# A two-layer trunk on one core: conditioning units ahead of the output units, and a first feed-forward unit on scaled x

## The chip, the core and the metric

The kernel runs on one core of a Trainium2 chip. The metric is the time of one launch in microseconds of the device (us), as the median of several runs. The profiles are single executions recorded by the hardware profiler. Five engines appear in them: PE (TensorE: matrix products; PEld is its weight load), DVE (VectorE), ACT (ScalarE), POOL (GpSimd) and SP (SyncE), which here only issues DMA transfers.

## What is computed

256 tokens of width 1024 pass through two layers. Each has a mixer and a feed-forward part, both behind an RMS norm that is modulated by a conditioning vector `c`, both added to the residual through a gate. The conditioning of a layer is one vector-matrix product, `silu(c) @ ada_w`, cut into six pieces.

```
mod = (silu(c) @ ada_w + ada_b); sh1, sc1, g1, sh2, sc2, g2 = split(mod, 6)
even layer:
  h = rms_norm(x, norm_mix) * (1 + sc1) + sh1
  a_val, a_gate, b_x, b_gate = split(h @ w_in, 4)
  ya = silu(layer_norm(conv31(a_val * sigmoid(a_gate))))     # causal, per channel
  yb = rg_lru(conv4(b_x)) * gelu(b_gate)                     # gated linear recurrence
  x = x + g1 * (concat(ya, yb) @ w_out)
  h = rms_norm(x, norm_ffn) * (1 + sc2) + sh2
  x = x + g2 * ((silu(h @ wg) * (h @ wu)) @ wd)              # width 2816
odd layer:
  short gated convolution and attention as mixer, then
  8 experts (width 3584), the best 2 of each token, as feed-forward
```

## The kernel before

All data is fp32. The tokens lie along the free dimension: `x` is [128 partitions, 8 blocks, 256 tokens]. The activations stay on the chip; what the DMA brings is weights, 469 MB in all.

**Weights come as a stream.** `stream_plan` (L56) lists all dense weights as units of 1 MB ([128, 2048]) in the order of their use: `cols` units (256 output columns of a projection), `rows` units (256 input rows), and conditioning units. SP issues one DMA a unit into a ring of ten buffers (`raw`; seven more come in for the experts). A buffer is given free when the unit that lay in it has been used, and only then the transfer for the unit ten places further down the plan can start. `S.step` takes the next unit of the plan, `S.take` hands out a prepared one, `S.prefetch(n)` prepares n units ahead, `S.look` is the number that `take` keeps prepared.

**Units are prepared in one of three ways.** Most are split into a high and a low part that PE can multiply at its fast rate (`part`, L368): ACT casts 512 columns to a high part (L375), DVE subtracts it from the weight for the low part (L376), into seven pairs of part buffers, four pairs a unit; a product is then three (L526 to L528: high by high, high by low, low by high). The units named in `WHOLE` are multiplied in fp32 as they lie (L549, L566), which the profile records as two matmuls a product. Conditioning units are of two kinds: `ada` ones are reduced on DVE (L476), `adap` ones on PE (L499, against `silu(c)`; fp32, so two records each), whose result, a row, is turned into columns by `turned_col` (L508): a copy on ACT, a transpose and an addition on DVE (L513, L514, L519).

**The order on each engine** is that of a scheduler: an instruction is placed as soon as its inputs allow, by the order of the code and by priorities (`high_priority`); each engine then runs its own list in order. `issue_after` ties an instruction behind another.

**The even mixer, where the change lies.** The input projection fills the blocks of the four branches (L549). The 31-tap convolution runs on two engines: 13 taps of a tile of 128 channels as products with diagonal matrices on PE (`conv_pe`, L834, diagonals made by ACT in L833), 18 on DVE (L846 to L850). The gates of the recurrence are products (L942), then ACT computes tanh, exp and square root (L945 to L952, L923, L925) and DVE multiplies and scans (`lru`, L920 to L930). `layer_norm_a` (L965) sums the convolution's four blocks over channels on PE (L968), centres them on DVE (L970), squares them on ACT (L627), sums again on PE (L611), takes the root, and broadcasts the scale over partitions on PE (L600); then it normalizes and splits (L979 to L982). The output projection has a half for the recurrence (32 products, L566, not dependent on the layer norm) and a half for the normed convolution (L526 to L528). Between the two halves stand twelve `adap` units (the pieces g1, sh2, sc2). `residual` (L709) adds each finished pair of blocks to x (L725), squares it and sums the squares on PE (L611).

**The even feed-forward.** `modulate` (L630) takes the root, broadcasts the norm's scale (L600), here with six further products that only keep PE busy (L595), and for each block multiplies on DVE (L656), scales and shifts on ACT (L657), casts on ACT (L660) and subtracts on DVE (L665). The loop at L1008 runs eleven times over a gate unit, an up unit and, one turn later, a down unit.

**The class `Early` (L669)** is used before the change at one place, the odd mixer's input. It uses that the norm's scale is one number a token and can be multiplied in after the product: `add` makes high and low parts of x times the column scale (ACT L683, DVE L684), `start` multiplies them with a weight unit while the norm's scale is still being computed (with two more columns for the shift, so 258 instead of 256), and `end` multiplies the product by the scale and adds the shift's part (L702 to L706).

**The experts.** Tokens are sorted by expert; groups of 32 rows, two or three groups an expert (`NGS`). `gather` fetches the rows of coming experts by products with a 0/1 matrix (L1449) while an earlier expert is being computed.

## Time and profile before

| | us |
|---|---|
| median of 3 runs (lowest, highest) | 1328.75 (1328.02, 1328.91) |
| the profiled execution, in all | 1330.99 |
| its span in the profile | 1329.2 |
| busy in it: PE, DVE, ACT | 1267.0, 466.4, 302.0 |
| granted clock of PE, mean share of full speed | 0.987 |

The profiled execution is 2.24 us longer than the median, and 1.8 us of it lie outside the span. Stages on its clock: input projection and conditioning until about 72 us, rest of the even mixer until 142, even feed-forward until 342, odd mixer until about 478, experts to the end. Where an engine's row shows "idle before", the name behind the arrow is what ended the idle time. The chain of waits is followed back from the last instruction; a piece in it is on the path that set the end.

### The profile page before, as it was taken

How to read it: one execution, taken by the hardware profiler on the slowest of the kernel's cores; microseconds unless marked ns; L12 is line 12 of the kernel's file. 1: busy time of each engine (PE TensorE's matmuls, PEld its weight loads, DVE VectorE, ACT ScalarE, POOL GpSimd, SP SyncE). 2: the span in 40 equal slices, each digit the busy share in tenths (PEclk: the TensorE clock that was granted, in tenths of full speed). 3: DMA queues.
4: the chain of work that ended last, by engine and by line, in shares of the span. 5: the costliest groups of instructions: out<-in, count | busy, mean ns of one | idle time of the engine just before them, and what ended most of it. 6: DMA issues, size and time to landing. Idle time of an engine off the chain costs nothing.

```text
span 1329.2 us, 30372 instructions
## 1 busy us (share of the span) xinstructions
PE 1267.0 (95%) x13194; PEld 755.7 (57%) x13194; DVE 466.4 (35%) x1025; ACT 302.0 (23%) x620; POOL 1.2 (0%) x23
## 2 busy tenths in 40 slices
PE   6979999999999999999989999999979999999975
PEld 5867899999988963453324453355313354345321
DVE  5894888888868431001011000101101101100100
ACT  3272654544746432000002000002001000100000
POOL 0000000000000000000000000000000000000000
PEclk8999899999999999999999999999999999999999
DMA  9936989898510769999999999999999999999995
GB/s 384 379 136 264 419 330 347 332 346 316 199 45 1 306 269 360 408 417 416 417 419 417 416 418 417 416 418 417 416 419 419 415 417 419 397 417 417 406 417 222
DMA packets 72220, 472.23 MB, mean 355 GB/s; under 512 B 8208, under 2 KB 10256, under 8 KB 27792
## 3 DMA queue, kind: packets, MB, share of 16 engines
q1 hardware_dynamic: 72080, 470.22, 87.8%
q8 instruction: 105, 1.72, 0.5%
q14 instruction: 35, 0.29, 0.1%
HBM read 469.14 MB, written 1.05 MB: 354 GB/s over the span
## 4 chain that ended last, share of the span: by engine, by line
PE 75%; DMA 20%; ACT 2%; DVE 2%; issue 1%; SPq 0%; ACTq 0%; DVEq 0%
DMA raw<-in_moe 20%; PE acc L1529 15%; PE mm L1529 14%; PE mm L1550 8%; PE mm L527 5%; PE mm L526 4%; PE mm L528 4%; PE mm L549 4%; PE acc L528 3%; PE acc L526 3%; PE acc L527 3%; PE acc L1550 3%; PE mm L499 1%; PE acc L566 1%; PE mm L1449 1%; PE acc L1543 1%
## 5 line engine op out<-in xcount | busy, mean ns | idle before, releaser
L1529 PE MATMUL acc<-raw,xe 128*32 128x512 f32 (+1 forms) x2688 | 259.2, 540 | 3.3 <-DMA raw<-in_moe 3.3
L1529 PE MATMUL mm<-raw,xe 128*32 128x512 f32 (+1 forms) x2688 | 257.8, 540 | 3.8 <-DMA raw<-in_moe 3.8
L1529 PEld LDWEIGHTS mm<-raw,xe 128*32 128x32 f32 x2688 | 86.5, 110 | 168.7 <-issue 154.4
L1529 PEld LDWEIGHTS acc<-raw,xe 128*32 128x32 f32 x2688 | 85.7, 110 | 164.0 <-issue 149.5
L376 DVE TENSOR_TENSOR wl<-raw,wh 128x512 fp32r<-128x512 f32 x204 | 136.3, 688 | 45.2 <-ACT wh L375 36.0
L375 ACT CAST wh<-raw 128x512 fp32r<-128x512 f32 x204 | 124.3, 621 | 115.5 <-PE mm L527 72.0
L527 PE MATMUL mm<-hlo,wh 128*128 128x256 f32 x496 | 141.2, 285 | 0.1
L526 PE MATMUL mm<-hh,wh 128*128 128x256 f32 x496 | 140.6, 284 | 0.0
L528 PE MATMUL mm<-hh,wl 128*128 128x256 f32 x496 | 140.1, 283 | 0.0
L1550 PE MATMUL mm<-raw,wh 128*32 128x256 f32 x2016 | 109.3, 379 | 0.0
L527 PEld LDWEIGHTS mm<-hlo,wh 128*128 128x128 f32 x496 | 94.9, 191 | 1.3 <-issue 0.9
L526 PEld LDWEIGHTS mm<-hh,wh 128*128 128x128 f32 x496 | 94.9, 192 | 1.0 <-issue 1.0
L528 PEld LDWEIGHTS mm<-hh,wl 128*128 128x128 f32 x496 | 94.8, 191 | 1.0 <-issue 1.0
L1665 DVE TENSOR_TENSOR wl<-wl,acc 128x512 f32<-128x512 f32 (+1 forms) x22 | 13.1, 597 | 226.5 <-PE acc L1529 226.5
L1550 PEld LDWEIGHTS mm<-raw,wh 128*32 128x32 f32 x2016 | 65.5, 110 | 43.9 <-issue 1.2
L476 DVE SCALAR_TENSOR_TENSOR raw<-raw,crow 128x1024 f32<-128x1024 f32 x64 | 77.5, 1219 | 1.9 <-DMA raw<-in_wst 1.9
L1665 DVE TENSOR_TENSOR wl<-wl,mm 128x512 f32<-128x512 f32 (+1 forms) x20 | 12.0, 598 | 188.4 <-PE mm L1529 188.4
L1550 PE MATMUL acc<-raw,wh 128*32 128x256 f32 x1344 | 72.9, 379 | 0.0
L1543 PE MATMUL acc<-raw,wh 128*32 128x512 f32 x448 | 53.0, 597 | 11.6 <-DMA raw<-in_moe 11.6
L1550 PEld LDWEIGHTS acc<-raw,wh 128*32 128x32 f32 x1344 | 43.7, 110 | 29.3 <-issue 0.8
L1662 ACT ACTIVATE wl<-mm 128x512 f32<-128x512 f32 (+1 forms) x22 | 12.0, 544 | 172.0 <-PE mm L1529 172.0
L1662 ACT ACTIVATE wl<-acc 128x512 f32<-128x512 f32 (+1 forms) x20 | 10.9, 544 | 171.9 <-PE acc L1529 171.9
(359 smaller groups left out, 1300.6 us busy)
## 6 DMA issues: line engine op xcount, KB each, us to landing
raw<-in_moe SPq DMA_DIRECT2D x236, 1024.0 KB, 19.8
raw<-in_wst SPq DMA_DIRECT2D x109, 1024.0 KB, 7.0
raw<-in_moe SPq DMA_DIRECT2D x128, 768.0 KB, 15.2
raw<-in_moe SPq DMA_DIRECT2D x8, 512.0 KB, 14.5
x<-in_xt SPq DMA_DIRECT2D x1, 1024.0 KB, 5.4
out<-x SPq DMA_DIRECT2D x4, 256.0 KB, 3.5
gw<-in_gates SPq DMA_DIRECT2D x1, 512.0 KB, 19.7
mask<-in_const SPq DMA_DIRECT2D x1, 192.0 KB, 5.0
```

Of the source, the lines that this page charges most:

```text
L375: self.nc.scalar.copy(h, t[:, j:j + PART])
L376: self.nc.vector.tensor_tensor(l, t[:, j:j + PART], h.bitcast(F32), op=OP.subtract)
L476: nc.vector.scalar_tensor_tensor(src, src, 1.0, crow, op0=OP.mult, op1=OP.mult, accum_out=raw_mod[pre][:, 2 * n + b:2 * n + b + 1])
L526: nc.tensor.matmul(o, wh, xh, start=first, stop=False, skip_group_check=skip)
L527: nc.tensor.matmul(o, wh, xl, start=False, stop=False, skip_group_check=skip)
L528: nc.tensor.matmul(o, wl, xh, start=False, stop=last, skip_group_check=skip)
L549: nc.tensor.matmul(o, wh, xh[:, k], start=(cb == 0 and k == 0), stop=(k == KB - 1), skip_group_check=True)
L1529: nc.tensor.matmul(ps[j * GROUP:(j + 1) * GROUP, :width], xe[:, k, r * GROUP:(r + 1) * GROUP], w[:, j * width:(j + 1) * width], start=(k = ...
L1543: nc.tensor.matmul(yb[0][t * GROUP:(t + 1) * GROUP], hs[r], w[:, f * D + h * 512:f * D + (h + 1) * 512], start=first, stop=last, skip_grou ...
L1550: nc.tensor.matmul(yb[c // 2][t * GROUP:(t + 1) * GROUP, c % 2 * 256:c % 2 * 256 + 256], hs[r], w[:, f * D + q * 256:f * D + q * 256 + 256 ...
L1662: nc.scalar.activation(h.bitcast(F32)[:, :width], ps[:, :width], AF.Silu)
L1665: nc.vector.tensor_tensor(h, h, ps[:, :width], op=OP.mult)
```

## The change

It has six parts. The twelve `adap` units stand ahead of the four output units in the plan and are taken ahead of `layer_norm_a`, and the splits of the two last output units are issued behind the centring. `turned_col` uses tiles of another name. In the first norm, the statistics are tied behind two of the first four `adap` units. The PE part of the convolution's last tile is issued after the recurrence. `Early` is used at the even mixer's end as well: the first gate unit is multiplied by scaled x, and the loop's first turn takes its result; the six warming products go. In the experts, the gather issued in expert 0 fetches the rows of expert 1 alone, and the later ones are shifted by one (before: 1 and 2, 3 and 4, 5 and 6, 7; after: 1, 2 and 3, 4 and 5, 6 and 7).

```diff
@@ stream_plan
     plan += [_cols("e_w_in", lo) for lo in (256, 768, 1024, 1280, 1536, 1792)]
+    plan += [("adap", "e", n) for n in range(4, 16)]
     plan += [_rows("e_w_out", lo) for lo in (512, 768, 0, 256)]
-    plan += [("adap", "e", n) for n in range(4, 16)]
@@ turned_col
-        t0 = turn_pool[0].tile([P, 512], F32, name="turn0")[:, :w]
-        t1 = turn_pool[0].tile([P, 512], F32, name="turn1")[:, :w]
+        t0 = turn_pool[0].tile([P, 2, T], F32, name="sg", bufs=2).rearrange("p b t -> p (b t)")[:, :w]
+        t1 = turn_pool[0].tile([P, 2, T], F32, name="sg", bufs=2).rearrange("p b t -> p (b t)")[:, :w]
@@ even mixer, first norm
-        sq = ev.tile([P, KB, T], F32, name="ri")
+        sq = ev.tile([P, KB, T + 2], F32, name="ri")[:, :, :T]
...
         st = Stats(ones_d, 1)
-        st.add(sq[:, 0])
+        for _ in range(2):
+            S.step()
+        with tc.issue_after(ada_last[0].ins):
+            st.add(sq[:, 0])
...
-        for _ in range(4):
+        for _ in range(2):
             S.step()
@@ even mixer, gates of the recurrence (g == 0)
-                conv_pe(3)
...
                 lru()
+                conv_pe(3)
                 S.pump(1000)
@@ layer_norm_a and the output projection
-                nc.vector.scalar_tensor_tensor(cv[:, b], ps[:, :T], -1.0 / MIX, cv[:, b],
-                                               op0=OP.mult, op1=OP.add)
+                centred = nc.vector.scalar_tensor_tensor(cv[:, b], ps[:, :T], -1.0 / MIX, cv[:, b],
+                                                         op0=OP.mult, op1=OP.add)
...
-
+            return centred
+
+        for _ in range(12):
+            S.step()
+        S.look = 0
+        S.prefetch(2)
         with tc.high_priority(offset=HIGH):
-            layer_norm_a()
-        S.prefetch(4)
-        S.look = 0
+            centred = layer_norm_a()
+        with tc.issue_after(centred.ins):
+            S.prefetch(4)
         banks = [acc_bank() for _ in range(4)]
         for g in range(2):
             proj_out(banks, None, None, 0, "e_w_out", g == 0, False, ge[:, 2 * g:2 * g + 2])
-        while S.plan[S.done][0] == "adap":
-            S.step()
         for g in range(2):
             if g == 1:
-                res, st = residual(banks, "e", 2, ev)
+                S.look = 2
+                first = Early(((ev, "ri"), (ev, "xsl")), "e", "e_norm_ffn", 3, 4)
+                res, st = residual(banks, "e", 2, ev, early=first)
             proj_out(banks, yh, yl, 2 * g, "e_w_out", False, g == 1 and res)
+        first.start("e_ffn_wg")
@@ even feed-forward
-        hh, hlo, _ = modulate(ff, st, "e", "e_norm_ffn", 3, 4, warm=WARM[0])
+        hh, hlo, rt = modulate(ff, st, "e", "e_norm_ffn", 3, 4)
...
-            pg = proj_in(hh, hlo, "e_ffn_wg", 0 if c else 4)
+            pg = proj_in(hh, hlo, "e_ffn_wg") if c else first.end(ff, rt)
...
-            pu = proj_in(hh, hlo, "e_ffn_wu")
+            pu = proj_in(hh, hlo, "e_ffn_wu", 0 if c else 4)
@@ experts
-    for e in range(0, NE - 1, 2):
-        gather(e, [n for n in (e + 1, e + 2) if n < NE])
+    gather(0, [1])
+    for e in range(1, NE - 1, 2):
+        gather(e, [e + 1, e + 2])
```

PE, around the layer norm's statistics and the broadcast of its scale (L600), before. `ge,raw` are the output projection's recurrence half, `raw,cact` conditioning, `ones_m,xr` statistics.

```order
L566 MATMUL acc<-ge,raw 128x256 x3
L968 MATMUL mm<-cv,one_pp 128x256
L566 MATMUL acc<-ge,raw 128x256 x4
L611 MATMUL mm<-ones_m,xr 128x1 x4
L566 MATMUL acc<-ge,raw 128x256
L611 MATMUL mm<-ones_m,xr 128x1 x2
L566 MATMUL acc<-ge,raw 128x256
L611 MATMUL mm<-ones_m,xr 128x1 x2
L566 MATMUL acc<-ge,raw 128x256 x6
L600 MATMUL mm<-sm_o,rs_788 128x128 x2
L566 MATMUL acc<-ge,raw 128x256 x17
L499 MATMUL mm<-raw,cact 32x512 x32
```

The same place after. L600 is again the broadcast.

```order
L499 MATMUL mm<-raw,cact 32x256 x9
L611 MATMUL mm<-ones_m,xr 128x1 x2
L499 MATMUL mm<-raw,cact 32x256 x2
L566 MATMUL acc<-ge,raw 128x256
L611 MATMUL mm<-ones_m,xr 128x1 x2
L566 MATMUL acc<-ge,raw 128x256
L611 MATMUL mm<-ones_m,xr 128x1 x2
L566 MATMUL acc<-ge,raw 128x256
L611 MATMUL mm<-ones_m,xr 128x1 x2
L566 MATMUL acc<-ge,raw 128x256 x6
L600 MATMUL mm<-sm_o,rs_892 128x128 x2
L566 MATMUL acc<-ge,raw 128x256 x23
```

Ahead of the broadcast stood 15 of the 32 output products and all conditioning behind the other 17; now 9 output products stand ahead and 23 behind, and the conditioning is all ahead.

DVE, from the even mixer's last residual to the first multiplication of the normal path (L656), before. `wl` are low parts of weights, `rs` the norm's scale.

```order
L725 SCALAR_TENSOR_TENSOR x<-acc,mod_e,x 128x256 x4
L376 TENSOR_TENSOR wl<-raw,wh 128x512 x2
L476 SCALAR_TENSOR_TENSOR raw,raw_e<-raw,crow 128x1024
L579 RECIPROCAL rs_1143<-rs_1143 128x2
L376 TENSOR_TENSOR wl<-raw,wh 128x512
L583 SCALAR_TENSOR_TENSOR rs_1143<-rs_1143 128x1 x2
L476 SCALAR_TENSOR_TENSOR raw,raw_e<-raw,crow 128x1024
L588 SCALAR_TENSOR_TENSOR rs_1143<-rs_1143 128x2
L476 SCALAR_TENSOR_TENSOR raw,raw_e<-raw,crow 128x1024
L656 TENSOR_TENSOR xr<-x,mm 128x256 x4
```

The same place after. `xsl` is the low part of the scaled x, `eb` the column of the shift's part, copied from the PSUM bank that the first feed-forward unit is summed in.

```order
L684 SCALAR_TENSOR_TENSOR xsl<-x,am,ri 128x256
L588 SCALAR_TENSOR_TENSOR rs_1253<-rs_1253 128x2
L684 SCALAR_TENSOR_TENSOR xsl<-x,am,ri 128x256 x2
L376 TENSOR_TENSOR wl<-raw,wh 128x512 x3
L704 COPY eb<-mm 128x1
L656 TENSOR_TENSOR xr<-x,mm 128x256 x4
L704 COPY eb<-mm 128x1
L376 TENSOR_TENSOR wl<-raw,wh 128x512
L665 TENSOR_TENSOR hlo<-xr,hh 128x256 x2
```

Between the norm's scale and L656 stood conditioning (L476); now the scaled x, three weight splits and the copy L704 stand there, which needs the finished first unit.

## Rows read from the trace of the kernel before

**Rows 1.** Stages: length; busy PE, PEld, DVE, ACT, POOL; PEclk; DMA share; GB/s.

```profile
72.00:102.00 30.00, 20.25 (x86) 16.46 (x84) 30.00 (x66) 20.41 (x35) 0.00 (x0) 0.90 0.21 74
142.20:151.15 8.95, 5.80 (x32) 5.66 (x32) 8.16 (x20) 3.41 (x10) 0.00 (x0) 0.58 1.01 416
361.00:442.00 81.00, 80.78 (x556) 68.24 (x554) 57.10 (x147) 42.66 (x102) 0.11 (x1) 0.98 0.13 47
478.00:600.00 122.00, 122.00 (x1552) 56.99 (x1552) 16.11 (x47) 14.48 (x34) 0.00 (x0) 1.00 0.96 382
600.00:678.00 78.00, 73.35 (x731) 24.57 (x734) 8.13 (x17) 3.73 (x9) 0.00 (x0) 1.00 1.01 417
```

**Rows 2.** Chain that ended last, 102 to 153 us: start, length, what.

```profile
102.04 0.96 PE mm L968 x2
...
110.55 7.34 PE acc L566 x34
117.89 9.59 PE mm L499 x112
...
128.62 1.00 PE mm L499 x16
...
142.23 0.88 DVE x L725 x2
...
147.74 1.20 PE mm L600 x4
...
152.40 0.21 PE mm L527
```

**Rows 3.** Timeline of PE, 72 to 112: start, length, instructions, idle before and releaser.

```profile
71.69 5.78 PE L834 MATMUL acc<-ya,dg 128*128 128x256 f32 x26
...
85.67 4.91 PE L549 MATMUL mm<-hh,raw 128*128 128x256 f32 x22
99.14 2.90 PE L566 MATMUL acc<-ge,raw 128*128 128x256 f32 x6 [8.56 <-issue]
```

**Rows 4.** Timeline of DVE, 98 to 128.

```profile
101.86 1.90 DVE L376 TENSOR_TENSOR wl<-raw,wh 128x512 fp32r<-128x512 f32 x3
...
125.58 0.71 DVE L514 STREAM_TRANSPOSE turn<-turn 128x512 f32<-128x512 f32 x1 [10.76 <-ACT turn L513]
```

**Rows 5.** Timeline of ACT, 72 to 98.

```profile
72.38 3.79 ACT L833 ACTIVATE dg<-sm_o,cwa 128x128 f32<-128x128 f32 x9
...
79.83 1.28 ACT L949 ACT_TABLE_LOAD   x1
81.12 0.60 ACT L949 ACTIVATE q<-ri,lah 128x256 f32<-128x256 f32 x1
```

**Rows 6.** Timeline of PE, first two feed-forward units and the third's start.

```profile
151.15 0.56 PE L526 MATMUL mm<-hh,wh 128*128 128x256 f32 x1
...
158.29 0.28 PE L526 MATMUL mm<-hh,wh 128*128 128x256 f32 x1
...
164.09 0.28 PE L526 MATMUL mm<-hh,wh 128*128 128x256 f32 x1
```

**Rows 7.** Timeline of PE, 336 to 362: odd mixer's end and scaled products.

```profile
341.46 0.28 PE L528 MATMUL acc<-yh,wl 128*128 128x256 f32 x1
...
344.18 0.48 PE L526 MATMUL mm<-xsh,wh 128*128 128x258 f32 x2
345.26 0.58 PE L527 MATMUL mm<-xsl,wh 128*128 128x258 f32 x1 [0.59 <-DVE xsl L684]
...
352.62 0.29 PE L528 MATMUL mm<-xsh,wl 128*128 128x258 f32 x1
```

**Rows 8.** Chain that ended last: two gathers of the expert stage.

```profile
508.58 4.54 PE mm L1449 x32
...
1138.87 3.72 PE mm L1449 x32
```

**Rows 9.** DMA issues from 40 to 130: count, KB each, median us to landing.

```profile
raw<-in_wst SPq DMA_DIRECT2D x25, 1024.0 KB, 13.9
```

More of the change, by code (lines that the diff above doesn't have):

```diff
@@ L766, in trunk @@
         nc.vector.tensor_scalar(gm, col("e_norm_mix", 0, KB), -0.5, None, op0=OP.mult)
-        hx = ev.tile([P, KB, T], F32, name="ri")
+        hx = ev.tile([P, KB, T + 2], F32, name="ri")[:, :, :T]
         hh = ev.tile([P, KB, T], F32, name="hh")
-        for _ in range(4):
+        for _ in range(2):
             S.step()
@@ L911, in trunk @@
                     tap(xb, bx, b, k, wcb, "e_conv_b_b", 4)
-        ri = ev.tile([P, 2, MB, T], F32, name="ri")
+        ri = ev.tile([P, KB, T + 2], F32, name="ri").rearrange("p b t -> p (b t)")[:, :KB * T]
+        ri = ri.rearrange("p (i b t) -> p i b t", i=2, b=MB)
         wt = ev.tile([P, MB, T], F32, name="bx")
```

## The prediction

> **What bounds the kernel now.** The reading goes from the whole to the place: which engine is busy in each stage, which chain of waits ends last there, and how long each piece of it is. TensorE (PE) is the engine that is full in most stages, but not in all [rows 1]. From 72 to 102 us VectorE (DVE) is busy 30.00 of 30 us and PE 20.25: the convolution and the recurrence are vector-bound. From 142.2 to 151.15 PE works 5.80 of 8.95 us at a granted clock of 0.58: that is the norm ahead of the feed-forward. In the expert stage, from about 600 us on, a DMA share of 1.01 at 417 GB/s says that the weights set the pace.
>
> Does an early gain reach the end? From 361 to 442 us PE is full (80.78 of 81) and the DMA share is only 0.13 [rows 1]: the ring of weight buffers is full and waits for PE. So whatever PE finishes earlier ahead of 442 lets every later transfer start earlier too, and the gain passes one for one. That is the assumption for the first two terms.
>
> The chain of waits names the pieces [rows 2]: behind the broadcast of the layer norm's scale, at 110.55, stand 17 output products (7.34 us; the profile records each fp32 product twice, x34), then 56 conditioning products (9.59 us), then the projection of the normed half, with eight more conditioning products inside it (1.00 us). It ends at 142.2, when the last residual starts (I call this moment P); then comes the norm's chain to the broadcast, 147.74 to 148.94. The first feed-forward product starts at 151.15 [rows 6].
>
> **The change part by part.** *Conditioning units ahead of output units.* The 64 conditioning products (9.59 + 1.00 = 10.6 us) go ahead of the layer norm's broadcast, into the vector-bound stretch. Behind the broadcast there now stand 23 output products, since nine instead of fifteen are ahead of it (the order shows this): 23 x 7.34/17 = 9.9 us. Before, 7.34 + 9.59 = 16.9 us stood there [rows 2]. That is 7.0 us, and with the 1.00 us that goes from inside the last part 8.0 us.
>
> What hides it: PE waits 8.56 us ahead of 99.14 [rows 3]. The stretch gets 10.6 us more and gives up six output products (6 x 0.43 = 2.6 us): 8.0 us into 8.56. It just fits, if the weights are there. Where it doesn't, the layer norm comes later, us for us. The last of its four sums on PE, which needs DVE's last block (102.04 [rows 2]), now stands behind 20 small conditioning products; 20 x 1.00/8 = 2.5 us would be lost if these ran only then.
>
> On DVE, a split step between the last block and the centring (three operations, 1.90 us [rows 4]) goes behind the centring, which releases perhaps 0.7 us of it; the transpose of the conditioning columns (0.71 [rows 4]) comes into this stretch, where DVE is full. I count the two against each other as zero. The third column tile of the convolution moves behind the recurrence: its nine ScalarE (ACT) diagonals (3.79 us [rows 5]) leave the front of ACT's chain, so the recurrence's inputs come up to 3.8 us earlier and the convolution's result later. DVE has other taps to fill with either way and is full, so this is zero too. The first norm's statistics, put behind two of the four first conditioning units, change the order on PE but not what must be done ahead of the broadcast: zero. Bounds of this part: 5.5 us (the 2.5 lost) to 8.8 us (the release on DVE without the transpose's cost).
>
> At ACT's chain the trace and a rule differ. In the trace a table load of 1.28 us starts at 79.83 and the next activation at 81.12 [rows 5], directly behind it. The Trainium skill, "ScalarE: Activation LUTs", section "What ACT_TABLE_LOAD costs", gives about 1.38 us of drain on top of each load; by it the three loads of this chain would put the diagonals behind it, and with them the convolution's last block, some 4 us later than I reckon, DVE would wait 2 to 3 us for that block, and the gain would be near 10, which lies in the range. The trace shows no such drain here, so the sum goes without.
>
> *First feed-forward unit while the norm is computed.* Before: first product 151.15, gate unit until 158.3, up unit until 164.1, 48 products each, which makes 0.12 us a product in the second and 1.3 us more in the first [rows 6]: 21.9 us from P. After: the gate unit runs on x scaled by column, before the norm's scale is known. The odd mixer already does this: its projection ends at 341.7, the first such product starts at 344.18 and the last at 352.62, ending about 352.7 [rows 7]: P + 11.0. But there the first 2.4 us go to statistics, and PE then waits 0.59 us for DVE's scaled rest [rows 7]. In the order of before, DVE had a weight split and a conditioning step between the residual and that rest; in the new order the rest stands right behind the residual, at the even mixer. I take the twin's 11.0 without the 2.4: P + 8.6, and 0.1 for the statistics that remain in between: P + 8.7.
>
> Then the new wait. On DVE a copy from the unit's PSUM bank stands ahead of the four multiplications that begin the normal path (the order shows it); it waits for all 48 products, and behind it is queued everything that the second unit needs. On ACT a weight cast waits likewise for part buffers that the unit frees at its end, and the normal path's activations stand behind it. So the second unit starts only after multiply, activation, cast: from the broadcast's end at 148.94 to 151.15, 2.2 us, in the trace of before [rows 2, 6]. Its 48 products take, as the gate unit's did with its slow start, 7.1 us: P + 8.7 + 2.2 + 7.1 = P + 18.0 against P + 21.9, 3.9 us. The six warming products go with it. Bounds: with the twin's 11.0 and 0.6 us more for the cast 1.0 us; 5.5 us if the second unit runs at 0.12 from its start and waits only 1.9 us.
>
> *Expert gather.* The gather in expert 0 shrinks from two experts' rows to one's, those that follow shift by one. A gather of the large form is 4.54 us on PE, of the small one 3.72 [rows 8]. In the stage of expert 0 PE is full (122.00 of 122 us [rows 1]) and the DMA share still under that of the later experts, so 0.8 us; later ones lie in stretches where DMA is the bound and cost nothing. Bounds: -1 (one more large gather in a place that PE sets) to 1.5.
>
> Sum: 8.0 + 3.9 + 0.8 = 12.7 us, 1.0%. The profiled execution took 1330.99 us (span 1329.2, 1.8 outside it), 2.24 above the median of 1328.75; the pieces are differences, so I take them off the median: 1316.0 us.
>
> **The rivals.** *B: the early unit gains almost nothing.* For it: after a pause PE runs at half clock in this trace: in the norm stretch the granted clock is 0.58, and a product of the gate unit then takes 0.21 us instead of 0.12 [rows 1, 2, 6]. The new order puts a second pause (the wait of 2.2 us) between two units. If the up unit then runs at 0.21 all through, 48 x 0.09 = 4.3 us are lost, 1.3 of which are in the 7.1 already. P + 18.0 + 3.0 + 0.6 for the cast = P + 21.6; 0.3 left, total 9.1: about 1319.6 us. Against: the twin's 11.0 has its own slow start in it and is over soon. The Trainium skill, "TensorE: Matmul & The Clock Gate", section "Loop structure matters more than you think", says that waits between matmuls decide whether they run warm; it speaks for this rival, and the 0.58 agrees with it. *C: the conditioning doesn't fit under the vector chain* and the layer norm comes 5 us later (weights that land late, 12 transfers in a ring of ten): 7.7 us gained, 1321.0 us. For it: transfers issued from 40 to 130 us took 13.9 us to land in the middle [rows 9], and the spare room on PE is half a us. Against: much of the 13.9 is queueing behind other transfers, and the DMA share in 72 to 102 is 0.21. *D: slower than before.* One mechanism: with ten buffers, the conditioning units 14 and 15 can only be fetched when PE has freed those of 4 and 5, and the layer norm's last sum stands behind 14 on PE. Before, PE ended its input products at 90.6 [rows 3]; the convolution's third tile (5.78 us [rows 3]), which stood ahead of them, moves behind them in large part, so unit 4's buffer comes free between 85 and 90. Landing 13.9 us later is 99 to 104, against 102.04, when the sum ran. Each us beyond costs one. It eats all 12.7 us only if the buffer comes free some 11 to 15 us later than that, and 3 us more give about 1332. Against: nothing in PE's new order there waits so long. *No effect at all* (1328.75): only if the expert stage's DMA went by its own clock, not by the ring; the share of 0.13 speaks against it. *E: more*, with the upper bound of each part: 8.8 + 5.5 + 1.5 = 15.8, below 1313.
>
> **How the numbers follow.** Forecast A, 1313 to 1318, 0.58; B 0.17; C 0.10; D 0.06; no effect 0.05; E 0.04. The range goes from just under A's end (1312.5) to C (1321.0) and leaves out D, no effect and E, 0.15. 0.2%, 2.7 us, is about what a measurement of this kernel can tell from no change. Faster by more than that: A, B, C and E, 0.89; within it: 0.05; slower: 0.06.
>
> **What would show it.** In the profile after: no conditioning products between the broadcast and the normed projection, which starts some 7 us earlier (near 120.5) and has no break; DVE still full from 72 to 102 us and PE's long wait there gone; layer norm broadcast still near 110 (C: near 115); P near 134. The last scaled product at P + 8.7, then a pause of about 2 us (B: followed by products 0.21 us apart to the end of the unit), the third unit at P + 18. Expert stage shifted by the same 12 us and still at 417 GB/s. Wrong would be: the shift shrinks in the expert stage, or DVE shows idle time before 100 us with PE or ACT as its releaser.

## The result and the profile after

The changed kernel takes 1316.32 us (median of 4 runs, 1315.62 to 1316.85); the kernel before took 1328.83 beside it (4 runs). The ratio is 0.9898, 95% interval 0.9886 to 0.9910: 12.5 us less, where 12.7 were forecast. The ratio is the recorded estimate with its interval and not quite the quotient of these two medians, which is 0.9906; between runs, ratios are compared with ratios. The profiled execution took 1316.23 us with a span of 1314.5. Line numbers after are 3 to 11 higher than before from the first norm of the even mixer on; those ahead of it (L376 to L725) are the same.

The stages of the profile after, with the columns of [rows 1]: PE is now busy 28.68 of 30 us from 72 to 102, where it had 20.25, and DVE is still full. The DMA works there (0.61 instead of 0.21). The stretch between the units of the feed-forward (143 to 152) has PE busy for 6.48 us at a granted clock of 0.81. Later stages are as before, moved forward.

```profile
72.00:102.00 30.00, 28.68 (x174) 17.29 (x176) 30.00 (x65) 20.08 (x36) 0.00 (x0) 1.00 0.61 228
...
143.00:152.00 9.00, 6.48 (x38) 5.80 (x38) 8.47 (x24) 8.98 (x22) 0.00 (x0) 0.81 0.33 117
...
466.00:588.00 122.00, 122.00 (x1563) 55.88 (x1566) 15.11 (x42) 12.66 (x28) 0.00 (x0) 1.00 0.97 390
588.00:666.00 78.00, 77.34 (x764) 29.81 (x760) 9.35 (x19) 8.16 (x21) 0.00 (x0) 1.00 1.01 417
```

The chain of waits after answers to [rows 2]: behind the broadcast of the layer norm's scale 23 output products in one piece, no conditioning behind them, then the norm's broadcast at 141.0 and products at 0.21 us each in the second unit.

```profile
112.08 9.93 PE acc L566 x46
...
140.99 0.44 PE mm L600 x4
...
148.82 0.21 PE mm L526
```

PE's timeline after, from 84 to 112 us (answers to [rows 3]): the wait of 8.56 us is gone, and the longest one left is 1.24 us, for a diagonal from ACT. Conditioning products stand between the convolution's, and 22 records of them (11 products) between the last sum L972 and the broadcast L600. DVE's row behind it is the convolution's last block: the last sum starts 0.06 us after its end.

```profile
84.70 1.90 PE L499 MATMUL mm<-raw,cact 128*32 128x512 f32 x10
...
87.60 1.06 PE L499 MATMUL mm<-raw,cact 128*32 128x512 f32 x8
89.90 2.00 PE L837 MATMUL acc<-ya,dg 128*128 128x256 f32 x8 [1.24 <-ACT dg L836]
...
103.01 0.70 PE L972 MATMUL mm<-cv,one_pp 128*128 128x256 f32 x2
103.64 1.48 PE L499 MATMUL mm<-raw,cact 128*32 128x256 f32 x18
...
105.58 0.62 PE L499 MATMUL mm<-raw,cact 128*32 128x256 f32 x4
...
111.47 0.61 PE L600 MATMUL mm<-sm_o,rs 128*128 128x128 f32 x4
```

```profile
102.53 0.42 DVE L961 TENSOR_TENSOR cv<-cv,odd 128x256 f32<-128x256 f32 x1
```

PE (first fence) and DVE (second) at the end of the scaled unit: the last of its products starts at 143.07, the second unit's first at 145.68, 2.33 us of PE's wait put down to ACT. On DVE the copy L704 waits for PE and the multiplication L656 stands behind it, as the prediction said.

```profile
143.07 0.28 PE L528 MATMUL mm<-ri,wl 128*128 128x258 f32 x1
145.68 0.35 PE L526 MATMUL mm<-hh,wh 128*128 128x256 f32 x1 [2.33 <-ACT hh L660]
```

```profile
143.03 0.16 DVE L704 COPY eb<-mm 128x1 f32<-128x1 f32 x1 [0.34 <-PE mm L528]
143.38 1.41 DVE L656 TENSOR_TENSOR xr<-x,mm 128x256 f32<-128x256 f32 x4 [0.19 <-PE mm L528]
```

The gather issued in expert 0 and the next one (in expert 1), from the chain: 3.71 us instead of 4.54 [rows 8] at the first. The next one fetches two experts of three groups each and takes 5.40 us; before, such a pair (experts 5 and 6) came only in expert 4.

```profile
495.60 3.71 PE mm L1459 x32
...
602.34 5.40 PE acc L1459 x32
```

**Where the time went.** The table gives the length of seven stages, each from the start of one named instruction to the start of the next, read from single profiles. A: to the first input product. B: to the layer norm's broadcast. C: to the last residual of the even mixer (P). D: to the third feed-forward unit. E: to the last residual of the feed-forward. F: to the first gather of all, which fetches expert 0's own rows. G: to the last PE instruction's end. Labels are those of the experiments below.

| profile | A | B | C | D | E | F | G | us |
|---|---|---|---|---|---|---|---|---|
| before | 20.9 | 89.0 | 32.3 | 21.9 | 177.7 | 136.5 | 842.3 | 1331.0 |
| gather alone | 21.8 | 89.2 | 32.3 | 20.8 | 177.7 | 134.2 | 841.4 | 1327.6 |
| changed | 20.4 | 91.1 | 24.0 | 18.2 | 178.5 | 133.1 | 840.9 | 1316.2 |
| last row turned late | 20.5 | 90.8 | 24.0 | 16.9 | 178.5 | 134.7 | 841.4 | 1316.8 |
| scaled unit alone | 21.3 | 89.7 | 32.3 | 17.9 | 178.6 | 133.2 | 842.1 | 1325.6 |
| the same again | 20.3 | 90.9 | 32.4 | 19.4 | 178.6 | 133.2 | 841.7 | 1326.8 |
| conditioning alone | 21.8 | 90.2 | 25.3 | 21.8 | 179.1 | 132.5 | 841.9 | 1322.9 |
| no scaled unit | 20.6 | 90.8 | 24.0 | 20.7 | 178.9 | 134.0 | 841.5 | 1321.4 |
| tile 3 at its old place | 20.6 | 94.2 | 25.3 | 19.6 | 178.6 | 132.4 | 841.1 | 1322.4 |
| the same again | 20.7 | 96.1 | 25.2 | 22.5 | 178.6 | 134.6 | 841.5 | 1329.6 |
| the same with filling | 20.9 | 90.8 | 24.0 | 16.8 | 178.8 | 134.6 | 840.8 | 1316.6 |

Against the two profiles that have nothing of the change ahead of the first gather (before, gather alone; up to there they are one program), the changed kernel is 0.9 us shorter in A, 2.0 longer in B, 8.3 shorter in C, 3.1 shorter in D, 0.9 longer in E, 2.2 shorter in F. In G the gather's order takes 1.4 from before. A and B scatter against each other: run 12, which has the old order there, has 20.3 and 90.9. E and F belong together: the changed order puts statistics of two more blocks inside the feed-forward's last unit (16 records ahead of its last products instead of 8), which ends E later and shortens the statistics that stand at the start of F.

### The profile page after: what moved, and what is told of

Same layout as the page of the kernel before. It is cut to its first block, busy times and chain, and to the rows that moved or that the text cites. A ratio compares the mean times of both kernels' runs of the same rounds, so it can differ in the third digit from the quotient of the medians.

```text
span 1314.5 us, 30367 instructions
## 1 busy us (share of the span) xinstructions
PE 1264.3 (96%) x13182; PEld 750.3 (57%) x13182; DVE 471.2 (36%) x1042; ACT 304.1 (23%) x630; POOL 1.2 (0%) x23
## 4 chain that ended last, share of the span: by engine, by line
PE 79%; DMA 14%; DVE 5%; ACT 1%; issue 0%; SPq 0%; ACTq 0%; DVEq 0%
PE acc L1539 18%; PE mm L1539 17%; DMA raw<-in_moe 12%; PE mm L1560 8%; PE acc L1560 6%; PE mm L527 4%; PE mm L526 4%; PE mm L528 4%; PE acc L526 3%; PE acc L528 3%; PE acc L527 3%; DMA raw<-in_wst 2%; PE acc L1459 1%; DVE cv L853 1%; DVE odd L853 1%; PE acc L566 1%
## 5 line engine op out<-in xcount | busy, mean ns | idle before, releaser
L376 DVE TENSOR_TENSOR wl<-raw,wh 128x512 fp32r<-128x512 f32 x204 | 135.6, 687 | 38.3 <-ACT wh L375 32.8
L526 PE MATMUL mm<-hh,wh 128*128 128x256 f32 x480 | 136.4, 284 | 2.3 <-ACT hh L660 2.3
L527 PE MATMUL mm<-hlo,wh 128*128 128x256 f32 x480 | 136.6, 285 | 0.2
L528 PE MATMUL mm<-hh,wl 128*128 128x256 f32 x480 | 136.0, 283 | 0.0
L526 PEld LDWEIGHTS mm<-hh,wh 128*128 128x128 f32 x480 | 91.9, 191 | 3.5 <-issue 3.5
L527 PEld LDWEIGHTS mm<-hlo,wh 128*128 128x128 f32 x480 | 91.9, 191 | 1.3 <-DVE hlo L665 0.7
L528 PEld LDWEIGHTS mm<-hh,wl 128*128 128x128 f32 x480 | 91.9, 191 | 0.7 <-issue 0.7
L476 DVE SCALAR_TENSOR_TENSOR raw<-raw,crow 128x1024 f32<-128x1024 f32 x64 | 76.7, 1218 | 2.4 <-DMA raw<-in_wst 2.4
L528 PE MATMUL acc<-yh,wl 128*128 128x256 f32 x176 | 49.8, 283 | 0.0
```

The lines of the kernel that those rows point to most:

```text
L376: self.nc.vector.tensor_tensor(l, t[:, j:j + PART], h.bitcast(F32), op=OP.subtract)
L476: nc.vector.scalar_tensor_tensor(src, src, 1.0, crow, op0=OP.mult, op1=OP.mult, accum_out=raw_mod[pre][:, 2 * n + b:2 * n + b + 1])
L526: nc.tensor.matmul(o, wh, xh, start=first, stop=False, skip_group_check=skip)
L527: nc.tensor.matmul(o, wh, xl, start=False, stop=False, skip_group_check=skip)
L528: nc.tensor.matmul(o, wl, xh, start=False, stop=last, skip_group_check=skip)
```

## The experiments

All times of a run are compared with the kernel before, run beside it on the same chip. In the diffs, "..." stands for lines left out.

**1. The scaled unit alone.**

```diff
(kernel before)
...
+                S.look = 2
+                first = Early(((ev, "ri"), (ev, "xsl")), "e", "e_norm_ffn", 3, 4)
-                res, st = residual(banks, "e", 2, ev)
+                res, st = residual(banks, "e", 2, ev, early=first)
...
+        first.start("e_ffn_wg")
...
-            pg = proj_in(hh, hlo, "e_ffn_wg", 0 if c else 4)
+            pg = proj_in(hh, hlo, "e_ffn_wg") if c else first.end(ff, rt)
...
-            pu = proj_in(hh, hlo, "e_ffn_wu")
+            pu = proj_in(hh, hlo, "e_ffn_wu", 0 if c else 4)
```

The tile names and sizes that the unit needs come with it, as in the change, and the six warming products go.

> The kernel before with the scaled first feed-forward unit alone; plan, convolution order and gather as before. Theory (the parts add up): the last residual starts at 142.2 us as before, the third unit starts 18.2 us after it instead of 21.9, so 3.7 us less in all, ratio 0.9972. Rival (the early unit's gain exists only behind the earlier projection, because it needs the conditioning columns to be long there): the last conditioning columns here arrive only in the projection's second half, the scaled rest waits, and 1 us or less is left, ratio 0.9992 or more.

Measured: 1328.4 us against 1329.56, ratio 0.9993 (0.9984 to 1.0002), eleven executions from 1325.6 to 1330.0. In its profile (1325.64) stage D is 17.9 us, as in the changed kernel. The median speaks for the rival's size, the profile for the theory's. Run 12, a second profile, and run 5 bear on this.

**2. The conditioning units alone.**

```diff
(kernel before)
+    plan += [("adap", "e", n) for n in range(4, 16)]
     plan += [_rows("e_w_out", lo) for lo in (512, 768, 0, 256)]
-    plan += [("adap", "e", n) for n in range(4, 16)]
...
+        for _ in range(12):
+            S.step()
+        S.look = 0
+        S.prefetch(2)
         with tc.high_priority(offset=HIGH):
-            layer_norm_a()
-        S.prefetch(4)
-        S.look = 0
+            centred = layer_norm_a()
+        with tc.issue_after(centred.ins):
+            S.prefetch(4)
...
-        while S.plan[S.done][0] == "adap":
-            S.step()
```

> The kernel before with the conditioning units ahead of the layer norm alone; no scaled unit, convolution and gather as before. 26 output products stand behind the broadcast here (23 in the changed kernel). Theory (the layer norm comes 1.5 us later, as in the changed kernel, because ScalarE's copy of the last conditioning row waits for PE between two squares): 16.9 - 26 x 0.43 = 5.7, plus 1.0 and about 0.3 in the projection's second half, less 1.5: 5.5 us, ratio 0.9959. Rival (the new place of the convolution's third tile is what makes room on PE): the last layer norm sum comes over 2 us later than the changed kernel's 103.0 and under 3.5 us are left, ratio 0.9974 or more.

Measured: 1323.47 us, ratio 0.9960 (0.9946 to 0.9973), 5.3 us less; 5.5 were expected. Stage B is 1.1 us longer and C 7.0 shorter than before. The last sum came at 102.65, not late, so the rival fell for this kernel. With the convolution at its old place PE waits 2.98 us here for DVE's last block, and the 18 conditioning records behind the wait still take 1.48 us, as in the changed kernel; half clock shows only later, in the six output products ahead of the broadcast, which take 4.52 us instead of 2.84 there.

```profile
102.65 0.70 PE L968 MATMUL mm<-cv,one_pp 128*128 128x256 f32 x2 [2.98 <-DVE cv L957]
103.28 1.48 PE L499 MATMUL mm<-raw,cact 128*32 128x256 f32 x18
```

**3. The gather alone.**

```diff
(kernel before)
-    for e in range(0, NE - 1, 2):
-        gather(e, [n for n in (e + 1, e + 2) if n < NE])
+    gather(0, [1])
+    for e in range(1, NE - 1, 2):
+        gather(e, [e + 1, e + 2])
```

> The kernel before with the new gather order alone. Theory: the gather in expert 0 takes 3.7 instead of 4.5 us on PE and 0.8 us pass to the end, ratio 0.9994; up to 478 us it is the kernel before, so its profile also shows which of the odd mixer's times of before belong to one run only. Rival: the transfers of the expert stage set the end anyway and the 0.8 us are lost in the waits at the ends of experts 1 and 4, ratio 1.0000.

Measured: 1328.34 us, ratio 0.9993 (0.9984 to 1.0002). The time can't tell 0.8 us from nothing. The traces can: stage G is 842.3, 842.1, 841.7 and 841.9 us in the four profiles with the old gather (mean 842.0) and between 840.8 and 841.5 in the seven with the new one in the table (mean 841.2). The difference is 0.8 us, as forecast. Up to the first gather this is the kernel before; its stage F is 2.3 us shorter than in the profile of before, so that much of [rows 1]'s odd mixer belonged to one execution.

**4. The last conditioning row turned into columns later.**

```diff
(changed kernel)
-            turned_col(mod[pre][:, lo:lo + w // 32], ps[:, :w], ...)
+            if n == 15:
+                S.turn_late = turn_now
...
+        with tc.issue_after(last_sq.ins):
+            S.turn_late()
```

> The changed kernel, with the last conditioning row turned into columns behind the four squares of the layer norm instead of between the second and the third. Theory (the copy's wait for PE delays the squares by 1.4 us and with them the whole rest up to the broadcast): the four squares run without a pause, the broadcast comes 1.4 us earlier, near 110.2, and the time falls by 1.4 us against the changed kernel, to 1314.9. Rival (PE's conditioning products ahead of the statistics set that moment): the broadcast stays at 111.5 and the time does not change by 0.5 us.

Measured: 1316.9 us (4 runs, 1314.6 to 1318.4), ratio 0.9906 (0.9891 to 0.9921). The rival holds. ACT's timeline has the four squares (line 634 here) in one piece and the copy (518) behind them; PE's shows that the statistics (616) nevertheless start at 104.88, behind nine conditioning products, and that two more stand in the middle. The broadcast (605) came at 111.30, 0.2 us earlier, and 8.46 us behind the last sum as in the changed kernel.

```profile
104.03 1.41 ACT L634 ACTIVATE xr<-cv 128x256 f32<-128x256 f32 x4 [1.38 <-DVE cv L981]
106.14 0.37 ACT L518 COPY sg<-mm 128x256 f32<-128x256 f32 x1 [0.70 <-PE mm L499]
```

```profile
103.47 1.48 PE L499 MATMUL mm<-raw,cact 128*32 128x256 f32 x18
104.88 0.61 PE L616 MATMUL mm<-ones_m,xr 128*128 128x1 f32 x4
105.41 0.62 PE L499 MATMUL mm<-raw,cact 128*32 128x256 f32 x4
...
111.30 0.61 PE L605 MATMUL mm<-sm_o,rs 128*128 128x128 f32 x4
```

**5. The changed kernel without the scaled unit.** The lines of run 1, taken out of the changed kernel, with the six warming products back.

> The changed kernel without the scaled first feed-forward unit (gate unit behind the norm, six warming products, as before); all else as changed. Theory: the third unit starts about 21.5 us after the projection's end instead of 16.9 to 18.2, so 3.8 us slower than the changed kernel, ratio to before 0.993 (about 1320 us). Rival (the scaled unit is worth about 1 us, as its run alone on the kernel before gave, since the second unit pays the pause back at half clock): ratio 0.991, about 1317.5 us.

Measured: 1320.85 us, ratio 0.9932 (0.9918 to 0.9946), against 0.9898 with the unit. As the theory had it: the unit is worth 4.5 us in the changed kernel by the two ratios. Stage D is 20.7 here.

**6. The third tile of the convolution back at its old place.**

```diff
(changed kernel)
             if g == 0:
+                conv_pe(3)
...
                 lru()
-                conv_pe(3)
```

> The changed kernel with the PE part of the convolution's third tile back ahead of the gates of the recurrence; all else as changed. Theory (VectorE is full either way and PE has the same work): the time from the first input product to the projection's end changes by under 0.7 us, ratio to before as the changed kernel's, 0.990 to 0.991. Rival (the move is what lets PE's conditioning fit): ScalarE's chain ends 3.8 us later, VectorE or PE waits for it, 2 us or more lost, ratio 0.992 or more.

Measured: 1326.67 us (eleven executions, 1322.4 to 1329.6), ratio 0.9978 (0.9969 to 0.9987). The theory fell, and by more than the rival asked: without this move, which I had put at zero, 10 of the 12.5 us are gone. PE's timeline of its profile shows the place. PE waits 3.80 us for DVE's last block, and then the same 18 conditioning records take 2.54 us instead of 1.48, the next four 1.07 instead of 0.62, and the broadcast comes at 114.80 instead of 111.47. The profile is that of one of the two fastest executions (1322.44 us), so it shows only some 6 of the 10 us.

```profile
102.74 0.70 PE L972 MATMUL mm<-cv,one_pp 128*128 128x256 f32 x2 [3.80 <-DVE cv L961]
103.37 2.54 PE L499 MATMUL mm<-raw,cact 128*32 128x256 f32 x18
...
106.78 1.07 PE L499 MATMUL mm<-raw,cact 128*32 128x256 f32 x4
...
114.80 0.61 PE L600 MATMUL mm<-sm_o,rs 128*128 128x128 f32 x4
```

**7. The first norm's statistics back ahead of the four units.**

```diff
(changed kernel)
-        for _ in range(2):
-            S.step()
-        with tc.issue_after(ada_last[0].ins):
-            st.add(sq[:, 0])
+        st.add(sq[:, 0])
...
-        for _ in range(2):
+        for _ in range(4):
             S.step()
```

> The changed kernel with the first norm's statistics back ahead of all four first conditioning units. Theory (the arrival of the fourth unit sets the start of the input projection, whatever the order): the first input product starts between 20.4 and 21.8 us, within what runs of one kernel differ, and the time does not change by 0.5 us. Rival (PE loses time at the front when the statistics come first, as the two profiles with the new order, 20.37 and 20.48, against 20.91 to 21.79 with the old one, suggest): first input product at 21.4 on average and 1 us slower, 1317.4.

Measured: 1317.02 us, ratio 0.9904 (0.9889 to 0.9919). The first input product starts at 21.64 here. With the old order it starts at 20.27 to 21.79 in six profiles (mean 21.3), with the new one at 20.37 to 20.93 in all eight (mean 20.7). So there may be 0.6 us in it and less scatter; the times can't tell it from zero.

**8. The pause in front of the second unit filled.**

```diff
(changed kernel)
         first.start("e_ffn_wg")
+        with tc.issue_after(last_mm[0].ins):
+            keep_warm(9, ident, ident)
```

> The changed kernel with nine further fp32 products of 128 columns on PE directly behind the scaled unit (their result is not used), which fill the pause of 2.3 us ahead of the second unit. Theory (the pause is what makes the granted clock fall in the second unit): no half clock in the second unit, its 48 products take 5.8 to 6.3 us instead of 6.6 to 7.9, about 1.2 us faster than the changed kernel, 1315.2. Rival (the clock there is set by the stretch ahead, not by the pause, or the products delay the second unit): second unit as long as before and 0 to 0.5 us slower.

Measured: 1316.35 us (4 runs), ratio 0.9899 (0.9884 to 0.9914), as the changed kernel. The filling stood where it should, on PE from 142.99, and the second unit ran at full clock.

```profile
142.99 2.17 PE L597 MATMUL acc<-sm_o 128*128 128x128 f32 x18
145.47 0.35 PE L528 MATMUL mm<-hh,wh 128*128 128x256 f32 x1 [0.32 <-issue]
```

But so it did in run 4 without any filling: the two rows below are the stretch 148 to 152 of the changed kernel (clock 0.63) and of run 4 (1.00). A pause of 2.3 us is followed by half clock in some executions and not in others, so this run can't show that the filling did it. Inconclusive.

```profile
148.00:152.00 4.00, 3.98 (x22) 3.98 (x23) 3.84 (x11) 3.98 (x10) 0.00 (x0) 0.63 0.00 0
```

```profile
148.00:152.00 4.00, 4.00 (x34) 4.00 (x35) 3.83 (x12) 4.00 (x11) 0.00 (x0) 1.00 0.00 0
```

**9. The wait of run 6 filled.**

```diff
(run 6)
+                if n == 14 and i == 1 and j == 0:
+                    fill_after[0] = ada_last[0]
...
             for b in range(MB):
+                if b == MB - 1:
+                    with tc.issue_after(fill_after[0].ins):
+                        keep_warm(13, ident, ident)
                 nc.tensor.matmul(ps[:, :T], one_pp, cv[:, b], ...)
```

> The run with the convolution's third tile back in its old place (1326.7 us), with 13 further fp32 products of 128 columns on PE (result not used) put into PE's wait of 3.8 us ahead of the layer norm's last sum. Theory (what the move of the convolution saves is PE's half clock after that wait, at a place where PE is the bound): conditioning products behind the last sum at full clock (1.5 us for 18 records instead of 2.5), broadcast about 3.3 us earlier than in that run, time 1321 us or less, ratio to before 0.994 or less. Rival (the wait itself or ScalarE's later chain costs the time): within 1.5 us of 1326.7, ratio 0.997 or more.

Measured: 1316.98 us (6 runs), ratio 0.9906 (0.9891 to 0.9922). Thirteen products without any use gave back 9.7 us of run 6's time: with the convolution at its old place this kernel is as fast as the changed one. PE's timeline: the filling from 99.36, a wait of 0.69 us, the conditioning records in 1.48 and 0.62 us again, broadcast at 111.69.

```profile
99.36 3.17 PE L599 MATMUL acc<-sm_o 128*128 128x128 f32 x26
103.22 0.70 PE L979 MATMUL mm<-cv,one_pp 128*128 128x256 f32 x2 [0.69 <-DVE cv L965]
103.85 1.48 PE L501 MATMUL mm<-raw,cact 128*32 128x256 f32 x18
...
105.80 0.62 PE L501 MATMUL mm<-raw,cact 128*32 128x256 f32 x4
...
111.69 0.61 PE L604 MATMUL mm<-sm_o,rs 128*128 128x128 f32 x4
```

One thing goes with it: the scheduler put 9 output products ahead of the broadcast here and 6 in run 6. That is stage C, 24.0 against 25.3 us; what is left of the difference stands in stages B (90.8 against 94.2) and D (16.8 against 19.6), where run 6 has half-clock products. The part in B follows the wait directly. In between, from 116 to 140 us, PE ran at full clock in both profiles of run 6, so how the wait reaches the scaled unit in D is not shown.

**10. Run 6 once more, for a second profile.**

> The run with the convolution's third tile in its old place once more, for a second profile, since its times spread from 1322.4 to 1329.6 and the profiled execution was one of the two fastest. Theory (the spread is how long PE stays at half clock after its pauses): every difference of over 0.5 us between the two profiles begins and ends in a stretch with half-clock products, and the rest of the stages agree within 0.5 us. Rival (transfers or waits differ): a stage without half clock differs by over 1 us.

Measured: one execution, 1329.56 us, 7.1 us longer than the first profile of the same program. Compared product by product, the two drift apart at four places only. In the input projection's first products it is 1.3 us. Near 103 us it is 0.4. In the scaled unit, 141.6 to 144.7 us on the first profile's clock, it is 2.9, and in the odd mixer's scaled unit (340 to 343) 2.3. Everywhere else the difference stays as it is, within 0.7 us. The windows of the two, each on its own clock, first run 6, then this run: the granted clock is 0.61 and 0.50 behind the wait, 0.87 and 0.74 around the scaled unit, 1.00 and 0.94 in the odd mixer.

```profile
103.00:116.00 13.00, 13.00 (x60) 9.42 (x60) 3.68 (x15) 4.89 (x11) 0.00 (x0) 0.61 1.01 419
...
143.00:156.00 13.00, 9.93 (x69) 9.55 (x69) 11.78 (x32) 10.63 (x25) 0.00 (x0) 0.87 0.61 243
...
340.00:400.00 60.00, 59.80 (x414) 52.10 (x413) 47.64 (x121) 38.11 (x81) 0.11 (x1) 1.00 0.20 73
```

```profile
103.00:116.00 13.00, 12.06 (x49) 8.12 (x50) 4.10 (x16) 4.93 (x10) 0.00 (x0) 0.50 1.01 420
...
143.00:156.00 13.00, 10.66 (x61) 10.20 (x59) 9.67 (x25) 8.51 (x21) 0.00 (x0) 0.74 0.35 101
...
340.00:400.00 60.00, 60.00 (x402) 53.95 (x402) 44.10 (x105) 37.02 (x78) 0.11 (x1) 0.94 0.27 96
```

And two neighbouring products in this run's scaled unit, 0.22 us apart, where run 6 has 0.12:

```profile
147.84 0.42 PE L527 MATMUL mm<-xsl,wh 128*128 128x258 f32 x1
148.06 0.42 PE L528 MATMUL mm<-ri,wl 128*128 128x258 f32 x1
```

So the theory holds for these two executions: what they differ by is how long PE stays at half clock.

**11. No wait for the scaled unit's end.**

```diff
(changed kernel; last_mod: the last multiplication and the last cast of the normal path)
+                with tc.issue_after(last_mod[0].ins):
                     nc.vector.tensor_copy(bias[:, cb:cb + 1], self.ps[cb][:, T:T + 1])
...
+            if c == 0:
+                with tc.issue_after(last_mod[1].ins):
+                    S.prefetch()
```

> The changed kernel with the copy from the first unit's bank tied behind the last of the norm's multiplications on VectorE, and the weight splits for the third unit tied behind the last cast of the normal path, so that neither waits for the scaled unit's end ahead of the second unit's data. Theory (the pause of 2.3 us is made by these two waits alone): the second unit starts within 0.8 us of the first one's end, the third unit 2 to 3.3 us earlier than 16.9 to 18.2 us after the projection's end, time 1313.0 to 1314.3, ratio 0.988 to 0.989. Rival (the path from the scale to the second unit's first block, 4 us and more behind the broadcast here, or the later splits of the third unit set the time): under 0.7 us gained, ratio 0.990.

Measured: 1318.34 us (5 runs), ratio 0.9916 (0.9903 to 0.9929), not faster. The copy and the casts were out of the way, and still the second unit started 2.40 us after the first one's end. DVE's timeline says why: the multiplication (658 here) now stands behind three weight splits and a conditioning step (476) that the scheduler put into the free place. PE then also ran the unit's products at half clock, after a second wait of 0.55 us.

```profile
141.19 1.89 DVE L376 TENSOR_TENSOR wl<-raw,wh 128x512 fp32r<-128x512 f32 x3
142.99 1.22 DVE L476 SCALAR_TENSOR_TENSOR raw<-raw,crow 128x1024 f32<-128x1024 f32 x1
...
144.14 1.41 DVE L658 TENSOR_TENSOR xr<-x,mm 128x256 f32<-128x256 f32 x4
```

```profile
143.45 0.28 PE L528 MATMUL mm<-ri,wl 128*128 128x258 f32 x1
146.13 0.41 PE L526 MATMUL mm<-hh,wh 128*128 128x256 f32 x1 [2.40 <-ACT hh L662]
147.09 0.58 PE L527 MATMUL mm<-hlo,wh 128*128 128x256 f32 x1 [0.55 <-DVE hlo L667]
```

So the two waits that the prediction named don't make the pause alone: the splits end at 143.08 here, and the copy stood at 143.03 in the changed kernel. What a free place on DVE would give is not shown, since the scheduler filled it.

**12. Run 1 once more, for a second profile.**

> The kernel before with the scaled unit alone once more, for a second profile: its first profile was its fastest execution (1325.6), the median of eleven is 1328.4. Theory (here, too, the spread is half clock, since PE keeps its waits of 7 to 8 us ahead of the layer norm and the scaled products start at whatever clock those leave): what this profile is slower by stands in stretches with half-clock products, the third unit still starts 16.9 to 22.5 us after the projection's end, the stages without half clock agree within 0.5 us. Rival (the conditioning columns, which come late in this kernel, make the scaled products wait): PE waits of over 1 us with DVE or ACT as releaser between the projection's end and the third unit, beyond the pause of 2.3 us.

Measured: one execution, 1326.81 us. Between P and the third unit PE has no wait over 0.2 us but the usual pause (2.0 us), so the rival falls. The longest waits of PE from 85 to 165 us:

```profile
PE acc L566 <- issue: 8.6, 1, 8.6
PE mm L526 <- ACT hh L660: 2.0, 1, 2.0
...
```

From P on this execution is slower than run 1's profile at one place, the scaled unit, where products are 0.21 us apart up to 148.5 (1.5 us; stage D 19.4 instead of 17.9). Stages E, F and G agree within 0.4. Both profiles are faster than the median of run 1, and no profile of its slower executions was caught: what those lose is not shown. That it is half clock behind PE's wait (6.9 and 8.6 us in the two profiles), which this kernel keeps, is the likely cause and no more.

## Why the prediction was right, and where it was not

The total came out 0.2 us from the forecast. That it came so near is in part luck: by the profiles the three terms are worth 7.6, 3.1 to 4.5 and 0.8 us, 11.5 to 12.9 together, and a part that the forecast put at zero decides whether two of them pay.

- **Conditioning ahead of the output units, 8.0 us: right in kind, some 0.4 too large.** Stage C got 8.3 us shorter, as 7.0 + 1.0 said, but the layer norm did not stay quite where it was. Since A and B scatter against each other, the moment itself says more: the broadcast starts at 109.9 to 111.2 us in the four profiles with the old order there (before, runs 1, 3 and 12) and at 111.3 to 111.9 in the seven that have the conditioning ahead and no long wait on PE (changed, runs 4, 5, 7, 8, 9, 11), 0.8 us later on average, and P comes 7.6 us earlier. "8.0 us into 8.56, it just fits" held: PE's waits from the first input product to the broadcast fell from 9.8 to 1.8 us.
- **The stretch up to the broadcast, 0: not quite zero.** First, DVE sets the last sum: in every one of the fourteen profiles it starts 0.05 to 0.06 us after the end of DVE's last block, and that comes 0.5 us later on average in the new order, as far as the scatter lets one say. Second, from the last sum to the broadcast PE works without a gap, 8.46 us in all seven profiles against 7.9 to 8.5 in the four. 11 conditioning products, in two groups of 1.48 and 0.62 us, stand there, and run 4 shows that ACT's copy and squares don't set it. Third, the conditioning takes longer on PE than the 10.6 us that were moved: in the trace before, four of its records start 0.007 us apart and the next four 0.41 to 0.43 us later (512 columns). A product has two records, so four products take two such steps. The new order cuts the 32 wide products into runs of 5, 4, 5 and 18, and the one or two products left over at a run's end take two steps as well: 20 steps of 0.43 us instead of 16, 1.7 us more. The Trainium skill, "TensorE: Matmul & The Clock Gate", section "Why this matters for your kernels", has such small products run side by side; the 0.007 us agrees.
- **The convolution's third tile, 0: wrong.** It was worth 10 us in the changed kernel (run 6). What was overlooked is who waits, not who is full: the prediction looked at DVE, which is full either way, and not at PE, which in the old place finishes its conditioning early and waits 3.80 us for DVE. The forecast had counted the conditioning into PE's wait as if the wait were then gone; without the move 3.80 us of it were left, directly ahead of a stretch in which PE is the bound, and half clock followed. Run 9 shows that the wait is the cause: filling it brings the time back, of which 1.3 us are the output products' order. The step that failed is "DVE has other taps to fill with either way and is full, so this is zero too". The total was right because the change holds both parts, so the clock that the forecast assumed without saying so was there. The 10 us are not all the move's own: without the scaled unit, the move is worth 3.7 us together with the statistics and the gather (run 5, 0.9932, against run 2, 0.9960). The rest is the scaled unit. It gains 4.5 us behind the moved tile; with the tile at its old place, adding it to run 2 with the statistics and the gather gave run 6, which is slower than run 2 (0.9978 against 0.9960).
- **The scaled unit, 3.9 us: right in size, but only together with the convolution's move.** P + 18.2 against P + 18.0 in the forecast; 0.9898 against 0.9932 without it (run 5). The 21.9 us of before are 20.7 to 21.9 in the four profiles without the unit, and the third unit starts at P + 16.8 to P + 18.2 in the changed kernel and runs 4, 7, 8 and 9. Inside it the scaled products ended at P + 7.8 instead of 8.7, and the second unit took 7.9 us instead of 7.1. The reason given for the pause was only half of it: copy and casts do wait, but without them the pause stays (run 11), with splits and a conditioning step in their place.
- **Gather, 0.8 us: right** by the traces, too small for the times to show.
- **First norm's statistics, 0: open,** up to 0.6 us.
- **The odd mixer: not in the sum.** F is 2.2 us shorter than in the two profiles of the same old program, but those differ by 2.3 among themselves and the changed kernels' by 2.3 too. Nothing of it is put down to the change.
- **Rivals.** B's mechanism is real but not for long: in the changed kernel's profile some eleven products of the second unit ran at 0.21 us, in runs 4, 7 and 8 none. C and D did not happen: the last sum is at 103.0 instead of 102.0, and DVE was busy 30.00 of 30 us from 72 to 102.
- **The table load.** ACT after shows the activation at 75.43 directly behind a load of 1.28 us from 74.13: no drain here either, as in [rows 5], so the sum rightly went without one. The Trainium skill, "ScalarE: Activation LUTs", section "What ACT_TABLE_LOAD costs", has one of about 1.38 us; the measurement decides.

```profile
74.13 1.28 ACT L952 ACT_TABLE_LOAD   x1
75.43 0.60 ACT L952 ACTIVATE q<-ri,lah 128x256 f32<-128x256 f32 x1
```

None of the kernels run is faster than the changed one beyond its interval; the nearest are run 8 (0.9899) and run 7 (0.9904).

## What to carry to other kernels

Look for the longest wait of the engine that is the bound right behind it, and ask what the change leaves of it: here moving work in paid in full only where the rest of the wait disappeared too (3.80 us left in run 6, 0.69 in run 9). A wait of PE costs its own length and, in some executions, what the products after it lose at half clock. A move that changes no engine's busy time can decide whether another part pays, so parts of one change should be tried by taking one out, not only by putting one in alone: alone the scaled unit and the conditioning gave 0.9993 and 0.9960, together with the convolution's move and the rest 0.9898.

## What the runs showed of the hardware

Executions of one program differed by up to 7.2 us (1322.4 to 1329.6, run 6), and where two profiles of one program were compared (runs 6 and 10, runs 1 and 12), most of the difference lay in products at half clock (0.21 instead of 0.12 us) behind a wait of PE or among statistics products of one column. How long this lasts changes from run to run: from 148 to 152 us, behind the pause of some 2.3 us ahead of the second unit, the granted clock was 0.63 in the changed kernel's profile, 0.50 in run 11's and 1.00 in those of runs 4, 7 and 9. A wait of 2.98 us in run 2 was followed by conditioning records at full clock (1.48 us for 18) and by output products at half clock only later, one of 3.80 us in run 6 by the conditioning at half clock (2.54). The widest spreads (7.2 us in run 6, 5.5 in run 9, 4.4 in run 1) are those of kernels with the scaled unit; run 9 has no long wait left, so such a wait is not needed for a wide spread.

Conditioning products use 32 columns of the array, and four of their records run side by side: 0.43 us a step at 512 columns. Four products, of two records each, take two steps, and so do one or two left over (rows of 1.06 us for 8 records and of 1.90 us for 10 in the changed kernel's profile).
